# VectorE in written order during the preparation of a hybrid layer, with the steps of three triangular inversions dealt out anew

## The chip, the cores and the metric

One Trainium2 chip, one core. The metric is the device time of one execution in microseconds (us); lower is better. Engines are named as in the profile: PE is TensorE, DVE VectorE, ACT ScalarE, POOL GpSimd, SP SyncE (here only an issuer of DMAs).

## What is computed

One layer of a diffusion backbone on 512 latent and 256 context tokens, width 1024, float32: a normed and modulated input is projected and split into 8 heads of 2-D neighbourhood attention and 8 heads of a bidirectional RWKV-7 scan; both are joined, projected and added to the input; then comes a mixture of 32 experts, two per token. The reference has the scan as a recurrence over tokens, for both directions:

```python
def step(S, inp):
    r_t, w_t, kk_t, akk_t, k_t, v_t = inp
    S = (S * w_t[:, :, None, :]
         - jnp.einsum('bhvk,bhk->bhv', S, kk_t)[..., None] * akk_t[:, :, None, :]
         + v_t[..., None] * k_t[:, :, None, :])
    return S, jnp.einsum('bhvk,bhk->bhv', S, r_t)
...
yx = jnp.concatenate([na_x, rw_x], axis=-1) @ w_out
x = x + mod_x[2] * yx
hx2 = modulate(rmsnorm(x, norm2_g[l]), mod_x[3], mod_x[4])
x = x + mod_x[5] * hier_moe(hx2, ...)
```

## The kernel before

The scan is done in chunks of 64 tokens. Within a chunk the tokens are coupled through a 64x64 triangular matrix, which has to be inverted: its two 32x32 diagonal blocks by forward substitution on DVE, the block between them by two products on PE. There are 4 head pairs x 2 directions x 12 chunks = 96 such matrices, and they go in three batches of 32.

The program has stages: the norm (to about 50 us of the span), the preparation `rwkv_prep` (to about 425 us), the scan with the attention worked in between its steps, the output projection, and the experts (from about 716 us to the end), which stream their weights from memory.

`rwkv_prep` (line 580) loops over the head pairs p = 0 to 3 with `rw_pair` (line 655). A pair has four units U0 to U3 (direction and half of the tokens). For a unit, `decay` issues four matmuls (psg, paf), a tanh on ACT and a scan on DVE (sig); `decayed` multiplies on DVE (the tiles b, AR, BK, af) and POOL; `coupling` has 48 matmuls (pmg), whose results DVE and ACT copy to ND and NO. Ahead of the units stand two chains of small DVE operations for the norms of keys (sn, 12 of them) and of attention heads (nst, 15), and the tile kk. The stages n = 2 to 6 of a pair run the units staggered: at stage n, `coupling` of U(n-3), `decayed` of U(n-2), `decay` of U(n-1).

Between these, PE gets filler: the rest of the input projection (`other_prep`, line 560), as groups of matmuls ip and ipn. A tile's results are evacuated by ACT and by DVE (ks, rs, vs, rot), and its weights are split into two halves by ACT (whi) and POOL (wlo). `fill(us)` deals out matmuls of so many nominal us, from `FILLS[p][i]` at the places of pair p; what is left over runs at the start of the scan. The matmuls for the modulation vectors (pm, which wait for the weights wm) are dealt out among the filler; what is left of them comes before the third inversion, `s.all(s.mods)`.

An inversion is a generator, `solve_a` (line 793): transpose of ND to Mc, a copy Tc on ACT, 30 steps of two DVE operations each (tmp, then Tc += tmp, each on what the one before wrote, 30 to 240 columns), and two transposes Ta and Tn. While a filler is dealt out, `solve_on` (line 261) advances it by one step for every RATE[p] nominal us. The first batch is complete in pair 1 (stage 4), the second in pair 2 (stage 5), the third in pair 3 (stage 6). `solve_b` (line 822) runs what steps are left and issues the first product (pp<-Tn,NO); `solve_c` (line 839) issues the second, whose result TT goes to memory for the scan. `SOLVE_B` says at which pair and stage that happens for the first two batches.

Order: PE's matmuls of the preparation keep the order in which the code is written. For the other engines a scheduler chooses the order, unless the engine's name is in `s.ordered` (class `Ordered`, line 203), which pins each of its instructions to the written order. In the preparation `s.ordered = E1_ORD`, an empty tuple.

Of the kernel before, what the change touches and what calls it, by code (L numbers as in the profile page):

```python
# [8 lines left out]
F32 = mybir.dt.float32  # L9
# [64 lines left out]
def by_row(t):  # L74

    v = t[:, 0:512].rearrange("p (r c) -> p r c", c=64)
    return v[:, 0:4], v[:, 4:8][:, ::-1]


def by_tile(t):  # L80

    v = t.rearrange("p (k h c) -> p h k c", h=2, c=64)
    return v[:, 0], v[:, 1]
# [88 lines left out]

FILL = (2.2, 2.2, 2.66)
PRE = 8  
E1_ORD = ()
SCAN_ORD = ('vector',)
ORD_TO = 1
KP_AT = 2
END_ORD = ()
HT_DVE = (4, 6, 7)  # L180
START_FILL = (0, 12)
FILLS = ((17.23, 9.32, 4.14, 4.14, 4.14, 4.14, 6.22), (14.0, 9.0, 4.1, 4.7, 4.0, 4.0, 6.0), (14.0, 9.0, 4.1, 4.7, 4.0, 4.0, 6.0), (4, 3.13, 3, 2.72, 3.13, 3, 0.0))  
END_FILL = (4, 2)  
RATE = {1: 1.5, 2: 0.8}
SOLVE_B = {(2, 3): (0, 0), (2, 4): (0, 1), (3, 3): (1, 0), (3, 4): (1, 1)}
FIRST = ('k0', 'r0', 'v0')
ITEMS = (('k1', 'r1', 'v1', 'nk0'), ('k2', 'r2', 'v2', 'nq0'), ('k3', 'r3', 'v3', 'nv0'), ('nk1', 'gd', 'nq1', 'nv1'))  
MODGAP = 3.43  
H1 = (3, 2, 0)
UPE = lambda nc: nc.vector  # L190
LAST = 16  
OUT_ORD = ('scalar',)
MOE_ORD = ('vector',)
LAST_PARTS = (256, 256, 256, 256)
# [33 lines left out]
class K:  # L228
# [22 lines left out]
    def fill(s, us):  # L251

        while us > 0 and s.filler is not None:
            c = next(s.filler, None)
            if c is None:
                s.filler = None
                return
            us -= c
            s.solve_on(c)
# [320 lines left out]
    def rwkv_prep(s):  # L580
        tc, nc, L, PA = s.tc, s.nc, s.L, s.PA
        with tc.tile_pool(name="pb", bufs=1, side="right", reuse_waits="tile") as PB:
            s.PB = PB
            s.strict = True
            s.ordered = E1_ORD
            s.kt, s.rt, s.pend = {}, {}, None
# [21 lines left out]
            s.last = s.filler  # L608
            s.fill(LAST)
            s.solve_b()  # L610
# [44 lines left out]
    def rw_pair(s, p):  # L655

        nc, PB, prm = s.nc, s.PB, s.prm
        k, r = s.kt[p], s.rt[p]
        fill = lambda i: s.fill(FILLS[p][i])

        kkc = prm[:, P_KK + p:P_KK + p + 1]
        sq = PB.tile([128, TOK], F32, name="sq", bufs=2)
        s.act(sq, k, AF.Square, scale=kkc)

        rk = PB.tile([128, TOK], F32, name="sq", bufs=2)[:, 0:512]
        for o, a, b in zip(by_tile(rk), by_row(r), by_row(k)):
            nc.gpsimd.tensor_tensor(o, a, b, ALU.mult)
        U = [(d, hf) for d in range(2) for hf in range(2)]
        st = [s.decay(p, d, hf) for d, hf in U[:1]]
        pn = s.ps((128, 12), tag='pr', name="pnk")  # L670
        for i in range(6):
            s.mm(pn[:, 2 * i:2 * i + 2], sq[:, 128 * i:128 * i + 128], s.ctb[:, B_HONE:B_HONE + 2])
        sn = PB.tile([128, 36], F32, name="sn")
        nc.vector.tensor_scalar(sn[:, 12:24], pn, 1e-24, None, op0=ALU.max)
        s.rsqrt(sn[:, 0:12], sn[:, 12:24], sn[:, 24:36])
        rex = PB.tile([128, 6, 128], F32, name="sq", bufs=2)
        s.act(rex.rearrange("p i (h f) -> p (i h) f", f=64), sn[:, 0:12, None].to_broadcast([128, 12, 64]))
        fill(0)
        pb = s.ps((128, 8), tag='pr', name="pbo")
        for i in range(4):  # L680
            s.mm(pb[:, 2 * i:2 * i + 2], rk[:, 128 * i:128 * i + 128], prm[:, P_RK + 2 * p:P_RK + 2 * p + 2])
        nc.vector.tensor_copy(s.bonus[:, :, 2 * p:2 * p + 2], pb.rearrange("p (a b) -> p a b", b=2))
        p0, p1 = s.transposed(rex.rearrange("p a b -> p (a b)"), 'pr', "pr")
        kk = PB.tile([128, TOK], F32, name="kk")
        nc.vector.scalar_tensor_tensor(kk[:, 0:512], k[:, 0:512], kkc, p0, op0=ALU.mult, op1=ALU.mult)
        nc.vector.scalar_tensor_tensor(kk[:, 512:768], k[:, 512:768], kkc, p1, op0=ALU.mult, op1=ALU.mult)
        fill(1)

        ab = []
        for n in range(2, 7):  # L690
            i = n - 2
            if 1 <= i:
                s.coupling(p, *U[i - 1], *ab[i - 1])
            if i < 4:
                ab.append(s.decayed(p, *U[i], st[i], k, r, kk))
            if i < 3:
                st.append(s.decay(p, *U[i + 1]))
            if n == 6 and p == 3:
                s.all(s.mods)
                s.all(s.solve_a(p, s.NO))  # L700
                s.fill(sum(END_FILL))
            if (p, n) in SOLVE_B:
                b, half = SOLVE_B[p, n]
                if half == 0:
                    s.solve_b()
                s.solve_c(b, half)
            if n == 6 and p < 3:
                s.up_load(p + 1)
            fill(n)
        if p < 3:  # L710
            s.fill(1e9)
# [54 lines left out]
    def coupling(s, p, d, hf, AR, BK):  # L766
# [13 lines left out]
        while c < 6:  # L780
# [7 lines left out]
            if u0 + n == 32 and p < 3:  # L788
                s.solving, s.due, s.rate = s.solve_a(p, s.NO), 0.0, RATE[p]
                next(s.solving)  # L790
# [31 lines left out]
    def solve_b(s):  # L822

        PB = s.PB
        s.all(s.solving or ())
        s.solving = False
        NO, Ta, Tn = s.inverse
        lo, hi = s.LO, s.HI
        s.P1 = PB.tile([128, 32, 32], F32, name="P1", tag="Tc")
        for z in range(2):  # L830
            pq = s.ps(tag='pr', name="pp1")
            for k in range(16):
                u = 16 * z + k
                for h in range(2):
                    s.mm(pq[hi[h], 32 * k:32 * k + 32], NO[lo[h], u], Tn[lo[h], u])
            for h in range(2):
                s.act(s.P1[hi[h], 16 * z:16 * z + 16].rearrange("p u c -> p (u c)"), pq[hi[h], :])

    def solve_c(s, b, z):

        nc, PB = s.nc, s.PB
        NO, Ta, Tn = s.inverse
        P1, lo, hi = s.P1, s.LO, s.HI
        TT = PB.tile([128, 16, 64], F32, name="TT", tag="Mc" if b == 2 and z else "TT")

        g0, parts = 32 * b + 16 * z, []
        g = g0
        while g < g0 + 16:
            n = min(12 - g % 12, g0 + 16 - g)
            parts.append((g // 24, g // 12 % 2, g % 12, g - g0, n))  # L850
            g += n
        pq = s.ps(tag='pr', name="pp2")
        for p, d, a, k0, n in parts:
            src = Tn if d else Ta
            ro = hi if d else lo
            for k in range(k0, k0 + n):
                u = 16 * z + k
                for h in range(2):
                    l, r = (Ta, P1) if d else (P1, Ta)
                    s.mm(pq[ro[h], 32 * k:32 * k + 32], l[hi[h], u], r[hi[h], u])  # L860
            us, ks = slice(16 * z + k0, 16 * z + k0 + n), slice(k0, k0 + n)
            for q in range(4):
                rr, o = slice(32 * q, 32 * q + 32), 32 * (q % 2)
                s.act(TT[rr, ks, o:o + 32], src[rr, us])
                if q % 2 != d:
                    nc.gpsimd.memset(TT[rr, ks, 32 - o:64 - o], 0.0)
        for p, d, a, k0, n in parts:
            ro, ks = hi if d else lo, slice(k0, k0 + n)
            for h in range(2):
                s.act(TT[ro[h], ks, (0 if d else 32):(32 if d else 64)],  # L870
                      pq[ro[h], 32 * k0:32 * k0 + 32 * n].rearrange("p (u c) -> p u c", c=32))
        for p, d, a, k0, n in parts:
            for x, y in s.runs(d, a, a + n, d):
                (s.nc.scalar if b == 2 else s.nc.sync).dma_start(s.at(s.TT, d, x, y)[:, :, d, p].rearrange("c p f -> p c f"),
                                                                 TT[:, k0 + x - a:k0 + y - a])
# [1153 lines left out]
```

## Time and profile before

| what | value |
|---|---|
| median of 3 runs | 1200.48 us (1197.87, 1200.48, 1200.89) |
| profiled execution, its own time | 1198.07 us |
| its span (the time axis of the trace) | 1196.3 us |
| mean granted clock of PE, 1.0 is full | 0.951 |
| busy share of the span: PE, DVE, ACT, POOL | 91%, 53%, 34%, 21% |
| memory read | 283.22 MB |

The busy share is a mean over stages with different limits. In this program it says little on the preparation, where PE, DVE and POOL hand work to each other, so the profile is read by stretches of time and by what each engine waited for.

### The profile page before, as it was taken

How to read it: one execution, taken by the hardware profiler on the slowest of the kernel's cores; microseconds unless marked ns; L12 is line 12 of the kernel's file. 1: busy time of each engine (PE TensorE's matmuls, PEld its weight loads, DVE VectorE, ACT ScalarE, POOL GpSimd, SP SyncE). 2: the span in 40 equal slices, each digit the busy share in tenths (PEclk: the TensorE clock that was granted, in tenths of full speed). 3: DMA queues.
4: the chain of work that ended last, by engine and by line, in shares of the span. 5: the costliest groups of instructions: out<-in, count | busy, mean ns of one | idle time of the engine just before them, and what ended most of it. 6: DMA issues, size and time to landing. Idle time of an engine off the chain costs nothing.

```text
span 1196.3 us, 23890 instructions
## 1 busy us (share of the span) xinstructions
PE 1091.7 (91%) x9673; PEld 762.6 (64%) x9674; DVE 633.8 (53%) x1384; ACT 403.2 (34%) x780; POOL 247.0 (21%) x283
## 2 busy tenths in 40 slices
PE   3899999969587689999998979999999999999996
PEld 1677777748466678888776754646464646464644
DVE  5745567986938523554578782333333333333335
ACT  3543546347373534555322251111111111120200
POOL 0664465524334100020253030000000000000000
PEclk9999999979878787999999989999999999999998
DMA  9544655446434278764353939999999999999995
GB/s 370 174 132 142 192 188 178 144 129 186 136 87 166 68 213 225 220 179 107 103 144 119 364 123 365 409 409 409 408 409 409 408 409 408 409 409 409 407 409 188
DMA packets 148797, 310.00 MB, mean 259 GB/s; under 512 B 32323, under 2 KB 71107, under 8 KB 148684
## 3 DMA queue, kind: packets, MB, share of 16 engines
q1 hardware_dynamic: 142860, 305.82, 71.4%
q10 hardware_dynamic: 5792, 2.62, 0.8%
q8 instruction: 77, 1.26, 0.4%
q14 instruction: 36, 0.29, 0.1%
q0 software_dynamic: 32, 0.00, 0.0%
HBM read 283.22 MB, written 25.17 MB: 258 GB/s over the span
## 4 chain that ended last, share of the span: by engine, by line
PE 65%; DVE 19%; DMA 7%; ACT 4%; issue 2%; POOL 2%; SPq 0%; ACTq 0%; DVEq 0%; POOLq 0%
PE ph L244 16%; PE py L244 8%; PE psc L244 7%; PE ip L244 7%; PE pga L244 4%; DMA wt<-in_w_dram 4%; PE ipn L244 4%; DVE Tc L213 4%; DVE tmp L213 3%; PE pgr L244 3%; PE pr L244 2%; PE pm L244 1%; PE ppt L248 1%; PE pon L244 1%; ACT TT L213 1%
## 5 line engine op out<-in xcount | busy, mean ns | idle before, releaser
L244 PE MATMUL ph<-wt,HS 128*64 128x512 f32 x1024 | 224.6, 593 | 0.4 <-DMA wt<-in_w_dram 0.2
L244 PEld LDWEIGHTS ph<-wt,HS 128*64 128x64 f32 x1024 | 73.5, 137 | 140.7 <-issue 126.4
L213 DVE TENSOR_TENSOR hid<-hid,ph 128x512 f32<-128x512 f32 x16 | 11.0, 688 | 249.6 <-PE ph L244 249.6
L244 PE MATMUL py<-wt,hid 128*64 128x256 f32 x1024 | 114.5, 381 | 0.0
L244 PEld LDWEIGHTS py<-wt,hid 128*64 128x64 f32 x1024 | 71.9, 137 | 40.3 <-issue 3.9
L213 POOL CAST two<-sel 128x128 fp32r<-128x128 f32 x32 | 8.6, 296 | 425.4 <-PE pbc L244 425.4
L213 POOL TENSOR_TENSOR wlo<-wraw,whi 128x512 fp32r<-128x512 f32 x54 | 72.4, 1343 | 111.4 <-ACT whi L213 107.7
L244 PE MATMUL ipn<-whi,hth 128*128 128x256 f32 x256 | 82.2, 321 | 13.6 <-DVE vs L213 9.9
L213 DVE TENSOR_TENSOR x<-psc,x 128x512 f32<-128x512 f32 (+1 forms) x136 | 78.6, 650 | 0.0
L244 PE MATMUL ipn<-wlo,hth 128*128 128x256 f32 x256 | 77.4, 302 | 0.0
L244 PE MATMUL ipn<-whi,htl 128*128 128x256 f32 x256 | 76.8, 300 | 0.0
L244 PE MATMUL ip<-hth,whi 128*128 128x512 f32 (+1 forms) x200 | 74.7, 374 | 1.4 <-ACT nr L213 1.3
L244 PE MATMUL ip<-htl,whi 128*128 128x512 f32 (+1 forms) x200 | 71.3, 357 | 0.7 <-DVE htl L213 0.7
L244 PE MATMUL ip<-hth,wlo 128*128 128x512 f32 (+1 forms) x200 | 71.3, 356 | 0.0
L244 PEld LDWEIGHTS ipn<-whi,hth 128*128 128x128 f32 x256 | 54.1, 211 | 22.2 <-issue 19.4
L244 PE MATMUL pga<-OH,xh 128*128 128x256 f32 x240 | 60.1, 291 | 0.9 <-DVE OH L213 0.9
L244 PE MATMUL pga<-OH,xl 128*128 128x256 f32 x240 | 59.2, 287 | 0.0
L244 PE MATMUL psc<-yh,oht 128*128 128x512 f32 (+1 forms) x136 | 54.5, 405 | 1.2 <-DVE x L213 0.8
L213 ACT ACTIVATE hid<-pth 128x512 f32<-128x512 f32 x16 | 9.6, 599 | 133.3 <-PE pth L248 133.3
L244 PEld LDWEIGHTS ipn<-wlo,hth 128*128 128x128 f32 x256 | 54.2, 212 | 0.0
L244 PEld LDWEIGHTS ipn<-whi,htl 128*128 128x128 f32 x256 | 54.2, 212 | 0.0
L244 PE MATMUL psc<-yl,oht 128*128 128x512 f32 (+1 forms) x136 | 51.4, 381 | 0.1
(351 smaller groups left out, 2235.9 us busy)
## 6 DMA issues: line engine op xcount, KB each, us to landing
wt<-in_w_dram SPq DMA_DIRECT2D x384, 512.0 KB
wm<-in_wmod_dram SPq DMA_DIRECT2D x48, 512.0 KB
wraw<-in_w_in_dram SPq DMA_DIRECT2D x30, 256.0 KB
wraw<-in_w_na_dram SPq DMA_DIRECT2D x24, 256.0 KB
BKj<-BKd SPq DMA_DIRECT2D x12, 512.0 KB
BKd<-BK SPq DMA_DIRECT2D x12, 384.0 KB
ARz<-ARd SPq DMA_DIRECT2D x16, 256.0 KB
wo<-in_w_out_dram SPq DMA_DIRECT2D x16, 256.0 KB
```

The source lines that it names most:

```text
L213: i = f(*a, **k)
L244: i = s.nc.tensor.matmul(out, l, r, start=start, stop=stop)
L248: i = s.nc.tensor.transpose(out, x, s.ident if ident is None else ident)
```

## The change

Five edits, none of which adds or takes away a computation:

- `E1_ORD` becomes `('vector',)`: DVE keeps the written order through the whole preparation.
- `RATE` becomes 1.2 for the first inversion (it was 1.5), stays 0.8 for the second, and gets an entry 0.7 for the third. The third inversion was issued as a whole at stage 6 of pair 3; now its steps are dealt out between fillers as those of the other two.
- `SOLVE_B`: the products of the second inversion move from stages 3 and 4 of pair 3 to stages 5 and 6.
- `FILLS[3]`: the first two fillers of pair 3 grow from 4 and 3.13 to 8 and 4 nominal us; `LAST`, the filler before the last product, shrinks from 16 to 12.
- `solve_b` keeps Ta, Tn and its product in `s.halved`, where `solve_c` reads them, since the third inversion may now start before the second's last product is made.

```diff
-E1_ORD = ()
+E1_ORD = ('vector',)
...
-FILLS = (..., (4, 3.13, 3, 2.72, 3.13, 3, 0.0))
+FILLS = (..., (8, 4, 3, 2.72, 3.13, 3, 0.0))
 END_FILL = (4, 2)
-RATE = {1: 1.5, 2: 0.8}
-SOLVE_B = {(2, 3): (0, 0), (2, 4): (0, 1), (3, 3): (1, 0), (3, 4): (1, 1)}
+RATE = {1: 1.2, 2: 0.8, 3: 0.7}
+SOLVE_B = {(2, 3): (0, 0), (2, 4): (0, 1), (3, 5): (1, 0), (3, 6): (1, 1)}
...
-LAST = 16
+LAST = 12
...
             if n == 6 and p == 3:
                 s.all(s.mods)
-                s.all(s.solve_a(p, s.NO))
+                s.all(s.solving or ())
+                s.solving, s.due, s.rate = s.solve_a(p, s.NO), 0.0, RATE[p]
+                next(s.solving)
                 s.fill(sum(END_FILL))
...
     def solve_b(s):
...
-        s.P1 = PB.tile([128, 32, 32], F32, name="P1", tag="Tc")
+        P1 = PB.tile([128, 32, 32], F32, name="P1", tag="Tc")
+        s.halved = Ta, Tn, P1
...
     def solve_c(s, b, z):
...
-        NO, Ta, Tn = s.inverse
-        P1, lo, hi = s.P1, s.LO, s.HI
+        Ta, Tn, P1 = s.halved
+        lo, hi = s.LO, s.HI
```

What this moves is seen in the order of instructions on the engines. First DVE in pair 2, where the results of the projection tile v (vs) are taken out of PE's accumulators while the first inversion runs (the last number of a row is the shape; a step's size tells which of the 30 it is). Before:

```order
L213 TENSOR_TENSOR tmp<-Mc,Tc 128x108
L213 SCALAR_TENSOR_TENSOR vs<-ip,prm,vs 128x511
L213 TENSOR_TENSOR Tc<-Tc,tmp 128x4x27
L213 SCALAR_TENSOR_TENSOR vs<-ip,prm,vs 128x511
L213 SCALAR_TENSOR_TENSOR b_2810<-af,kk 128x384
L213 SCALAR_TENSOR_TENSOR sig<-cut,sig 128x390
L213 SCALAR_TENSOR_TENSOR vs<-ip,prm,vs 128x255
L213 TENSOR_TENSOR tmp<-Mc,Tc 128x84
L213 SCALAR_TENSOR_TENSOR vs<-ip,prm,vs 128x255
```

With the change:

```order
L213 TENSOR_TENSOR Tc<-Tc,tmp 128x7x24
L213 SCALAR_TENSOR_TENSOR b_2707<-af,kk 128x384
L213 SCALAR_TENSOR_TENSOR AR<-kk,Ep 128x6x64
L213 SCALAR_TENSOR_TENSOR BK<-b_2707,Em 128x6x64
L213 TENSOR_TENSOR af<-af,ks 128x384
L213 SCALAR_TENSOR_TENSOR sig<-cut,sig 128x390
L213 SCALAR_TENSOR_TENSOR vs<-ip,prm,vs 128x511 x2
L213 SCALAR_TENSOR_TENSOR vs<-ip,prm,vs 128x255 x2
L213 TENSOR_TENSOR tmp<-Mc,Tc 128x150
```

The four vs operations stood after the first operation of the step with 108 columns (the 27th); now they stand after the step with 168 columns (the 24th), but behind b, AR, BK, af of U0 and the scan sig of U1, and nothing stands between them.

Next DVE where the first inversion ends (Ta, Tn), at stage 3 of pair 2. Before:

```order
L213 TENSOR_TENSOR tmp<-Mc,Tc 128x30
L213 TENSOR_TENSOR Tc<-Tc,tmp 128x30
L213 STREAM_TRANSPOSE Ta<-Tc 128x32x32
L213 TENSOR_TENSOR ND<-pmg,ctb 128x192
L213 STREAM_TRANSPOSE Tn<-Tc 128x32x32
L213 SCALAR_TENSOR_TENSOR b_3072<-af,kk 128x384
L213 SCALAR_TENSOR_TENSOR sig<-cut,sig 128x390
```

With the change:

```order
L213 SCALAR_TENSOR_TENSOR AR<-kk,Ep 128x6x64
L213 SCALAR_TENSOR_TENSOR BK<-b_2825,Em 128x6x64
L213 TENSOR_TENSOR af<-af,ks 128x384
L213 SCALAR_TENSOR_TENSOR sig<-cut,sig 128x390
L213 TENSOR_TENSOR tmp<-Mc,Tc 128x84
L213 TENSOR_TENSOR Tc<-Tc,tmp 128x3x28
L213 TENSOR_TENSOR tmp<-Mc,Tc 128x58
L213 TENSOR_TENSOR Tc<-Tc,tmp 128x2x29
L213 TENSOR_TENSOR tmp<-Mc,Tc 128x30
L213 TENSOR_TENSOR Tc<-Tc,tmp 128x30
L213 STREAM_TRANSPOSE Ta<-Tc 128x32x32
L213 STREAM_TRANSPOSE Tn<-Tc 128x32x32
L213 TENSOR_TENSOR ND<-pmg,ctb 128x192
```

Before, the last steps and Ta stood ahead of ND of unit U0, and Tn right behind it. Now ND of U0 comes first, three steps and both transposes come last, and b, AR, BK, af of U1 and sig of U2 stand between.

Then PE in pair 3, at the first products of the second inversion (pp<-Tn,NO). Before:

```order
L244 MATMUL pmg<-AR,BK 32x64 x24
L244 MATMUL psg<-th_538,uph 128x384
L244 MATMUL psg<-th_538,upl 128x384
L244 MATMUL paf<-ad_613,uph 128x384
L244 MATMUL paf<-ad_613,upl 128x384
L244 MATMUL pp_3713<-Tn,NO 32x32 x32
L244 MATMUL pp_3748<-Tn,NO 32x32 x32
L244 MATMUL pp_3784<-Ta,P_3712 32x32 x8
L244 MATMUL pp_3784<-P_3712,Ta 32x32 x24
```

With the change:

```order
L244 MATMUL ip<-hth_111,wlo 128x512
L244 MATMUL pmg<-BK,AR 32x64 x24
L244 MATMUL pp_3961<-Tn,NO 32x32 x32
L244 MATMUL pp_3996<-Tn,NO 32x32 x32
L244 MATMUL pp_4032<-Ta,P_3960 32x32 x8
L244 MATMUL pp_4032<-P_3960,Ta 32x32 x24
L244 MATMUL ip<-hth_112,whi 128x512
```

The products stood behind pmg of unit U0 and the matmuls of `decay` for U2; now they stand behind pmg of U2, two stages later. Of the pm matmuls that were left over before the third inversion, a quarter has moved up among the fillers.

## Rows read from the trace of the kernel before

**Rows 1.** The page: the chain that ended last, share of the span by engine.

```profile
PE 65%; DVE 19%; DMA 7%; ACT 4%; issue 2%; POOL 2%; SPq 0%; ACTq 0%; DVEq 0%; POOLq 0%
```

**Rows 2.** Windows: stretch, its length, busy of PE, PEld, DVE, ACT, POOL; PEclk, DMA share, GB/s.

```profile
198.70:252.90 54.20, 44.91 (x361) 35.43 (x360) 52.97 (x110) 24.63 (x52) 28.25 (x27) 0.91 0.55 169
252.90:264.50 11.60, 8.34 (x81) 6.04 (x81) 11.43 (x21) 3.70 (x8) 1.65 (x3) 0.66 0.37 106
284.40:332.40 48.00, 31.09 (x297) 26.60 (x295) 46.26 (x102) 20.49 (x43) 17.12 (x25) 0.82 0.50 152
332.40:366.40 34.00, 27.30 (x514) 20.26 (x514) 11.65 (x25) 21.28 (x45) 12.29 (x22) 0.80 0.39 114
366.40:403.50 37.10, 28.75 (x191) 26.14 (x189) 35.49 (x80) 12.83 (x23) 13.38 (x11) 0.87 0.29 100
448.10:462.10 14.00, 14.00 (x138) 12.54 (x140) 3.38 (x10) 5.01 (x10) 0.00 (x0) 0.50 0.96 240
720.00:960.00 240.00, 239.25 (x1472) 132.09 (x1470) 84.14 (x137) 37.20 (x66) 4.28 (x16) 1.00 1.02 407
```

**Rows 3.** Waits of PE, whole span: us in total, times, longest.

```profile
PE pp L244 <- DVE Tn L213: 14.8, 2, 13.9
PE ipn L244 <- DVE vs L213: 9.9, 2, 9.7
PE pp L244 <- DVE nst L213: 5.7, 1, 5.7
PE pm L244 <- DMA wm<-in_wmod_dram: 4.2, 2, 3.5
PE pon L244 <- DMA V<-NVd: 3.9, 3, 1.8
...
PE pr L248 <- ACT sq L213: 3.1, 1, 3.1
```

**Rows 4.** Timeline of PE: start, duration, instruction, in brackets the wait before it.

```profile
254.66 0.55 PE L244 MATMUL ipn<-whi,hth 128*128 128x256 f32 x1 [9.75 <-DVE vs L213]
...
264.55 1.64 PE L244 MATMUL pp<-Tn,NO 32*32 32x32 f32 x92 [0.89 <-DVE Tn L213]
...
283.04 0.87 PE L244 MATMUL pmg<-BK,AR 64*32 64x64 f32 x48
...
332.54 1.67 PE L244 MATMUL pp<-Tn,NO 32*32 32x32 f32 x55 [13.95 <-DVE Tn L213]
```

**Rows 5.** Timeline of DVE at the first inversion's end.

```profile
254.89 0.97 DVE L213 TENSOR_TENSOR_SCAN sig<-cut,sig 128x390 f32<-128x390 bf16 x1
...
260.26 2.00 DVE L213 STREAM_TRANSPOSE Ta<-Tc 128x1024 f32<-128x1024 f32 x1
...
262.51 1.98 DVE L213 STREAM_TRANSPOSE Tn<-Tc 128x1024 f32<-128x1024 f32 x1
264.37 0.56 DVE L213 SCALAR_TENSOR_TENSOR b<-af,kk 128x384 f32<-128x384 f32 x1
```

**Rows 6.** Timeline of DVE, 216 to 305 us: start, duration, instruction; two mixed, two dependent.

```profile
217.47 0.37 DVE L213 TENSOR_TENSOR tmp<-Mc,Tc 128x210 f32<-128x210 f32 x1
217.76 0.17 DVE L213 TENSOR_TENSOR nst<-nst 128x16 f32<-128x16 f32 x1
...
304.62 0.41 DVE L213 TENSOR_TENSOR Tc<-Tc,tmp 128x240 f32<-128x240 f32 x1
305.06 0.41 DVE L213 TENSOR_TENSOR tmp<-Mc,Tc 128x240 f32<-128x240 f32 x1
```

**Rows 7.** Timelines of DVE and POOL, 244 to 251 us: start, duration, instruction.

```profile
247.59 1.31 DVE L213 TENSOR_TENSOR Tc<-Tc,tmp 128x198 f32<-128x198 f32 x1
...
250.26 0.35 DVE L213 TENSOR_TENSOR Tc<-Tc,tmp 128x184 f32<-128x184 f32 x1
...
247.30 2.72 POOL L213 TENSOR_TENSOR wlo<-wraw,whi 128x512 fp32r<-128x512 f32 x2
```

**Rows 8.** Groups of DVE, 366 to 403 us: instruction, count, busy us, mean ns, idle before.

```profile
L213 DVE SCALAR_TENSOR_TENSOR rot<-ip,prm,rot 128x511 f32<-128x511 f32 x2 | 1.5, 740 | 0.0
```

More of the change, by code (lines that the diff above doesn't have):

```diff
@@ L181 @@
 START_FILL = (0, 12)
-FILLS = ((17.23, 9.32, 4.14, 4.14, 4.14, 4.14, 6.22), (14.0, 9.0, 4.1, 4.7, 4.0, 4.0, 6.0), (14.0, 9.0, 4.1, 4.7, 4.0, 4.0, 6.0), (4, 3.13, 3, 2.72, 3.13, 3, 0.0))
+FILLS = ((17.23, 9.32, 4.14, 4.14, 4.14, 4.14, 6.22), (14.0, 9.0, 4.1, 4.7, 4.0, 4.0, 6.0), (14.0, 9.0, 4.1, 4.7, 4.0, 4.0, 6.0), (8, 4, 3, 2.72, 3.13, 3, 0.0))
 END_FILL = (4, 2)
-RATE = {1: 1.5, 2: 0.8}
-SOLVE_B = {(2, 3): (0, 0), (2, 4): (0, 1), (3, 3): (1, 0), (3, 4): (1, 1)}
+RATE = {1: 1.2, 2: 0.8, 3: 0.7}
+SOLVE_B = {(2, 3): (0, 0), (2, 4): (0, 1), (3, 5): (1, 0), (3, 6): (1, 1)}
 FIRST = ('k0', 'r0', 'v0')
@@ L836, in solve_b @@
             for h in range(2):
-                s.act(s.P1[hi[h], 16 * z:16 * z + 16].rearrange("p u c -> p (u c)"), pq[hi[h], :])
+                s.act(P1[hi[h], 16 * z:16 * z + 16].rearrange("p u c -> p (u c)"), pq[hi[h], :])
     def solve_c(s, b, z):
         nc, PB = s.nc, s.PB
-        NO, Ta, Tn = s.inverse
-        P1, lo, hi = s.P1, s.LO, s.HI
+        Ta, Tn, P1 = s.halved
+        lo, hi = s.LO, s.HI
         TT = PB.tile([128, 16, 64], F32, name="TT", tag="Mc" if b == 2 and z else "TT")
```

## The prediction

> **What bounds the kernel.** I read the page first: the chain that ended last runs over PE for 65% of it, DVE for 19% and DMA for 7% [rows 1]. A share says nothing on where, so the table of windows comes next. In the experts' stage DMA is occupied throughout at 407 GB/s (share 1.02) [rows 2]: its length is given by the bytes, nothing there can absorb or repay a delay, and what the preparation gains or loses arrives at the end. In the preparation the table of waits shows what PE lacked. The largest have DVE at their end: 14.8 us for Tn, 9.9 us for vs, 5.7 us for what the profile calls nst (Tn of the third inversion ends beside it) [rows 3]. The reader is to see in the windows that DVE is full just there: 52.97 of 54.2 us in the stretch that holds the first inversion, 46.26 of 48.0 in the second, 35.49 of 37.1 in the third [rows 2]. So the change is priced at the places where PE waits for DVE: what stands ahead of the awaited instruction in DVE's stream before, and what with the change. Durations are those of the profiled execution, 1198.07 us.
>
> **Evacuation of vs, pair 2.** PE waits 9.75 us, until 254.66 [rows 4]. DVE never rests, so the wait moves by the work put ahead of vs. The scheduler had run ahead to the 27th step by then; in written order DVE does the 24 that the fillers have dealt out. Two whole steps less are four operations near 0.4 us, -1.6. The written order puts b, AR, BK, af of one more unit behind Mc, where the scheduler had them before it: four operations, b lasting 0.56 us [rows 5], starts some 0.5 apart, +2.1; the scan of U1 (0.97) stands ahead now, +1.0. The third part is lost mixing. A step's operations depend on each other: tmp of 305.06 starts 0.03 us after Tc ended at 305.03. Independent ones overlap: nst of 217.76 starts 0.08 us before tmp ends [rows 6]. Before, 27 small operations (sn, nst) stood between steps and cost little more than the overlap left open; in written order they are a chain of their own, at 0.17 us each and the gap about 0.2 us, 5.4 in all. About half of that was paid before: +2.5. The first result is +4.0. DVE is also held up by POOL here (a step's operation takes 1.31 us while wlo is made on POOL and 0.35 when it is over [rows 7]), and which steps meet it will change; six such collisions, about 1 us each, either way give -2 to +10.
>
> The Trainium skill (VectorE: DVE Perf Modes, section "The DRAIN you can't avoid") says that the pipeline empties behind each DVE operation before the next one starts, and that chaining without waits does not avoid it. By that mixing never saved anything, and the term of 2.5 (and its like below) would be zero. The trace does not agree in full: the mixed operations do overlap by 0.08 us [rows 6].
>
> **First inversion's end, stage 3 of pair 2.** Before, PE's first product waited only 0.89 us [rows 4], since the scheduler put Tn (262.51) right behind ND and left sig of U2 to follow. With the written order ND of U0 comes, which needs pmg, then b, AR, BK, af of U1 (2.1), sig of U2 (1.0, after its tanh), the last three steps (six operations of 30 to 84 columns, where one of 210 takes 0.37 [rows 6]: some 0.25 each with the gaps, 1.5), Ta 2.00 and Tn 1.98 [rows 5], all in front of PE's product, which itself stands ahead of all later PE work. Sum from 262.6: 8.5 us, Tn ends at about 271, the product starts at about 271 where it was 264.55: +6.4. If sig runs while b to af do not hold it up and mixing costs nothing, +4; with POOL in the way, +8.
>
> **From pair 2's third unit to the third inversion.** This stretch runs from pmg at 283.04 [rows 4] to the first step at 366.4: the windows of 48.0 and 34.0 us. PE is busy 31.09 + 27.30 = 58.4, DVE 46.26 + 11.65 = 57.9 of these 82 us [rows 2]; neither fills it, the hand-offs do. Before, PE stood 13.95 us ahead of the second product [rows 4] and 3.1 ahead of pr (for sq and the sn chain behind it) [rows 3]. The product now stands behind pmg of U2, and the larger fillers stand where PE had run dry, so these 17.05 go. New waits come: pmg of U0 needs AR and BK, which now stand behind the steps dealt out before them (3.2 in my walk of both streams), pmg of U2 the same (3.5), and Tn stands behind the nst chain, two units' groups and a scan (2.4): 9.1. Mixing lost between steps and small operations is another 3. -17.05 + 9.1 + 3 = -5.0. The ends: if PE gets no new wait, what is gained is 17.05 less the added filler, 4.87 nominal us, -12; if every wait returns in another place, +2. The DMA waits of pm, 4.2 [rows 3], stay, since the rest of pm still stands behind the last unit.
>
> **Third inversion.** It was issued as a whole, but its fillers ran beside it, and DVE was full for 35.49 of 37.1 us [rows 2]; dealing its steps out cannot shorten it. The evacuations rot and gs of tile gd move ahead (rot 1.5 us for its two operations [rows 8], gs, half as wide, some 0.6: -2.1); the nst chain of tile nq1 now stands in the middle of the steps and waits for PE and ACT there (+2). Net 0, with ends -2 and +3. PE has 4 nominal us less to do meanwhile, so its wait for the last Tn grows from 5.7 to 10 or more; that lies beside DVE's work, which sets the end.
>
> **The scan's start.** The left-over filler stands before the first scan products, no longer partly behind; nothing is saved in work, but V, for which PE waited 3.9 us [rows 3], is asked for later relative to its store. Behind those waits PE ran at a granted clock of 0.50, the 1.2 GHz level, for 14.0 us [rows 2]; at 2.4 GHz this would be at most 7.0 shorter. So the relief lies between 0 and 3.9 + 7.0, some -10; I take -4: most of the waits, little of the clock.
>
> **The clock elsewhere.** Around the wait for vs the granted clock was 0.66 [rows 2]. Longer idle stretches before the first product cost a little more of this: +1 (0 to +3). Pairs 0 and 1 have no PE wait of note: 0. The `s.halved` edit issues nothing.
>
> **Sum.** 4.0 + 6.4 - 5.0 + 0 - 4.0 + 1.0 = +2.4, hence 1198.07 + 2.4 = 1200.5. The profiled execution lies 2.4 us under the median of the three runs, 1200.48, and near their lowest, so the forecast is no difference that can be measured: 0.3%, 3.6 us, is about what a measurement of this kernel tells from no change (1196.9 to 1204.1).
>
> **Rivals.** First, faster: *V and the clock.* If V arrives in time the scan's start goes at full clock (-10 instead of -4), and if pair 3's new waits stay small (-9 instead of -5), the sum is -7.6: 1190.5. For it: two of the largest waits end in one place, pair 3, and PE's product is moved away from there. Against: what PE no longer waits for there it waits for elsewhere, since DVE's work is the same. Chance 0.23.
>
> Second, faster: *unmixing is free.* Then 2.5 and 3 fall out: 1198.07 - 3.1 = 1195.0. For it: the scheduler's order was no optimum, it ran steps ahead of vs. Against: the 0.08 us overlaps. The rule of the Trainium skill quoted above (VectorE: DVE Perf Modes) would give this time. Chance 0.12.
>
> Third, slower: *head of line in pair 2.* In written order one instruction that waits for PE or ACT stops DVE, which in turn is what PE waits for; each such stop in the two stages around the first inversion's end costs both. It decides if ND or sig blocks before the steps are done: vs +9, first product +8, pair 3 at -5, the scan at -4, clock +2: +10, 1208. Against: rate 1.2 leaves only three steps there. Chance 0.22.
>
> Fourth, *no effect*: the order pinned is what ran already; excluded in pair 2 by the order shown, but the gains and losses may cancel to within a microsecond, 1200. Chance 0.05.
>
> **How the numbers follow.** The forecast has 0.38: 0.27 in the band, 0.06 faster, 0.05 slower. The two fast rivals add 0.23 and 0.12, of the latter 0.02 in the band; the slow one 0.22; no effect 0.05 in the band. Faster 0.39, same 0.34, slower 0.27. The terms' half-widths (6, 2, 7, 2.5, 5, 1.5) taken as independent give 11; so 1188 to 1211, which holds the fast rivals and the slow one.
>
> **What would show it.** Right: PE's wait for vs in pair 2 near 14 us; a wait of 6 to 8 us ahead of pp<-Tn in pair 2; no wait near 14 in pair 3, but two or three of 2 to 4; the third inversion still near 37 us with DVE full; a wait of PE of 10 or more at its end; waits for V under 3.9. Wrong, if vs is taken out earlier than before, if the first product finds Tn ready, or if the third inversion's steps start later than they did.

## The result, and the profile after

The changed kernel takes 1231.05 us (median of 4 runs, 1229.2 to 1237.2), the kernel before 1200.68 (median of 4 runs beside them). The ratio is 1.026, with a 95% interval of 1.022 to 1.031: slower by 2.6%, some 31 us. The forecast was no difference, 1200.5, in a range to 1211.

The page's row on busy time:

```profile
PE 1090.1 (89%) x9673; PEld 761.2 (62%) x9674; DVE 634.5 (52%) x1384; ACT 402.2 (33%) x780; POOL 247.1 (20%) x283
```

PE's busy time is what it was (1090.1 us; 1091.7 before); its share fell because the span grew to 1227.4. So no work was added; what came on top is waits. The table of what PE waited for (us in total, times, longest):

```profile
PE pp L244 <- DVE Tn L213: 23.0, 3, 12.7
PE psg L244 <- DVE upl L213: 15.9, 3, 6.6
...
PE ipn L244 <- DVE vs L213: 11.6, 3, 10.1
PE pmg L244 <- DVE BK L213: 11.4, 2, 9.2
PE pm L244 <- DMA wm<-in_wmod_dram: 8.3, 1, 8.3
PE pnt L248 <- ACT nx L213: 6.3, 1, 6.3
```

Against [rows 3]: Tn costs 23.0 us where it was 14.8, and in three places. The wait for vs is nearly the same. Two entries are new, 15.9 us for upl and 11.4 for BK; the wait for wm (4.2 before) and that for nx ahead of the scan (pnt, 3.2 before) have doubled. Where the lag comes about is seen when the same instruction is looked up in both timelines:

| instruction | before | after | lag |
|---|---|---|---|
| PE: pnk of pair 1 | 151.39 | 159.79 | 8.4 |
| PE: pnk of pair 2 | 210.41 | 229.02 | 18.6 |
| PE: first ipn behind vs, pair 2 | 254.66 | 275.22 | 20.6 |
| PE: first product of the first inversion | 264.55 | 292.34 | 27.8 |
| PE: pmg of U2, pair 2 | 283.04 | 312.77 | 29.7 |
| PE: pnk of pair 3 | 293.55 | 326.91 | 33.4 |
| DVE: first step of the third inversion | 366.36 | 401.23 | 34.9 |
| PE: first product of the third inversion | 403.53 | 437.99 | 34.5 |
| PE: first matmul of the experts (ph) | 716.34 | 747.16 | 30.8 |

18.6 of the 31 us are there at pnk of pair 2, before the first place that the prediction priced. The places in PE's timeline (start, duration, instruction, in brackets the wait before it):

```profile
150.99 0.44 PE L244 MATMUL psg<-th,uph 128*128 128x384 f32 x1
...
157.94 0.69 PE L244 MATMUL psg<-th,upl 64*128 64x384 f32 x1 [6.50 <-DVE upl L213]
...
159.79 2.72 PE L244 MATMUL pnk<-ctb,sq 128*128 128x2 f32 x12
...
227.17 0.69 PE L244 MATMUL psg<-th,upl 64*128 64x384 f32 x1 [6.57 <-DVE upl L213]
...
275.22 0.55 PE L244 MATMUL ipn<-whi,hth 128*128 128x256 f32 x1 [10.11 <-DVE vs L213]
...
292.34 3.46 PE L244 MATMUL pp<-Tn,NO 32*32 32x32 f32 x122 [8.71 <-DVE Tn L213]
...
373.94 1.51 PE L244 MATMUL pmg<-BK,AR 64*32 64x64 f32 x48 [9.22 <-DVE BK L213]
...
398.38 1.08 PE L244 MATMUL pm<-wm,scc 128*32 128x256 f32 x8 [8.35 <-DMA wm<-in_wmod_dram]
...
437.99 3.46 PE L244 MATMUL pp<-Tn,NO 32*32 32x32 f32 x122 [12.71 <-DVE Tn L213]
```

The two matmuls of `psg` stand one behind the other, and the second, whose weights are upl, waits 6.5 us at the boundary from pair 0 to 1 and 6.57 at the next. Behind these waits PE runs slower: `pnk`, 12 small matmuls, takes 2.72 us, where it took 1.50 at both places before; the granted clock from 157.94 to 165.00 us is 0.50, the 1.2 GHz level, and was 1.00 from 140.0 to 150.5.

Why upl is late is seen on DVE, at the boundary from pair 0 to pair 1:

```profile
150.73 0.69 DVE L213 TENSOR_REDUCE nst<-nx 128x8 f32<-128x512 f32 x1 [0.88 <-ACT nx L213]
151.73 1.28 DVE L213 TENSOR_REDUCE nst<-nx 128x8 f32<-128x512 f32 x2 [0.32 <-ACT nx L213]
153.05 1.49 DVE L213 TENSOR_SCALAR nst<-nst 128x24 f32<-128x24 f32 x3
...
156.41 0.35 DVE L213 TENSOR_TENSOR ND<-pmg,ctb 128x192 f32<-128x192 f32 x1
156.67 2.40 DVE L213 TENSOR_TENSOR upl<-row,uph 64x256 fp32r<-64x256 f32 x2
```

nst, the chain of a norm of the attention heads, started once ACT had its input (nx), and its first operations are to be seen here. Behind it come ND of U3 (156.41) and upl (156.67). In the code the filler whose last tile needs that norm stands at stage 5 and `up_load` at stage 6, and the order of DVE is now the code's. In the kernel before, the scheduler had made upl 7 us ahead of PE's use of it at 150.28:

```profile
142.34 0.86 DVE L213 TENSOR_TENSOR upl<-row,uph 64x256 fp32r<-64x256 f32 x2
```

At the next boundary it had made it just in time: the two operations of upl, one for each direction, ran from 207.62 to 209.43 us, and PE's first matmul with upl started at 209.30 without a wait.

The windows of the stretches of [rows 2], here from 208.5 to 437.95 (columns as there):

```profile
208.50:273.50 65.00, 47.84 (x361) 37.77 (x360) 55.50 (x110) 26.11 (x53) 26.82 (x26) 0.82 0.41 132
273.50:292.30 18.80, 8.41 (x81) 6.28 (x81) 13.57 (x25) 5.83 (x13) 5.11 (x7) 0.59 0.37 109
312.70:401.20 88.50, 65.46 (x832) 52.27 (x830) 66.49 (x132) 46.96 (x95) 34.68 (x43) 0.80 0.49 147
401.20:437.95 36.75, 23.84 (x233) 22.32 (x232) 32.87 (x76) 8.40 (x17) 11.25 (x16) 0.83 0.20 58
```

The stretch that holds the first inversion's steps up to vs, 54.2 us before, takes 65.0, and DVE is busy for 55.50 of it, where it was for 52.97: it is not full any more, it waits. (This stretch contains the boundary to pair 2.) The granted clock is 0.82 there (0.91 before) and 0.59 from vs to the first product. The third inversion takes 36.75 us as against 37.1, with DVE at 32.87.

### The profile page after: what moved, and what is told of

Same layout as the page of the kernel before. It is cut to its first block, busy times and chain, and to the rows that moved or that the text cites. A ratio compares the mean times of both kernels' runs of the same rounds, so it can differ in the third digit from the quotient of the medians.

```text
span 1227.4 us, 23886 instructions
## 1 busy us (share of the span) xinstructions
PE 1090.1 (89%) x9673; PEld 761.2 (62%) x9674; DVE 634.5 (52%) x1384; ACT 402.2 (33%) x780; POOL 247.1 (20%) x283
## 4 chain that ended last, share of the span: by engine, by line
PE 44%; DMA 10%; DVE 5%; ACT 2%; SPq 1%; POOL 1%; issue 1%; ACTq 0%; DVEq 0%; POOLq 0%
PE ph L244 15%; PE py L244 7%; DMA wt<-in_w_dram 7%; PE psc L244 5%; PE pga L244 4%; PE pgr L244 2%; PE acc L244 2%; PE pr L244 1%; PE ppt L248 1%; PE pon L244 1%; PE po L244 1%; DMA V<-NVd 1%; DVE x L213 1%; SPq L213 1%; DVE fst L213 1%
## 5 line engine op out<-in xcount | busy, mean ns | idle before, releaser
L244 PE MATMUL ipn<-whi,hth 128*128 128x256 f32 x256 | 80.1, 313 | 12.1 <-DVE vs L213 11.6
L213 ACT ACTIVATE S<-S,m 128x512 f32<-128x512 f32 x64 | 45.3, 717 | 26.7 <-DVE m L213 26.6
```

The lines of the kernel that those rows point to most:

```text
L213: i = f(*a, **k)
L244: i = s.nc.tensor.matmul(out, l, r, start=start, stop=stop)
```

## The experiments

A ratio is the kernel's time over that of the kernel before on the same chip, with its 95% interval. Theory A says that the written order makes the loss, theory B that the redistribution of steps, products and fillers does. An inversion has a first and a second product; where an expectation writes "the second product", with its wait of 14 us, the first product of the second inversion is meant (13.95 us before, [rows 4]).

**The order alone.** The kernel before, and in it only

```diff
-E1_ORD = ()
+E1_ORD = ('vector',)
```

> Kernel before with one edit: DVE in written order. Theory A (the written order itself makes the loss: small chains nst stand ahead of upl at the pair boundaries, b to sig ahead of Tn at the first inversion's end): slower by 22 to 40 us, 1223 to 1241, with waits of PE for upl near 15 us in all and a wait near 8 us at the first product; as the second product stays at its old place, its wait stays over 10 us. Theory B (the redistribution of steps, products and fillers makes the loss, the order little): within 5 us of before, no waits for upl.

Measured: 1250.24 us, ratio 1.039 (1.034 to 1.044). Slower still than the change, beyond theory A's range. Its waits of PE:

```profile
PE pp L244 <- DVE Tn L213: 29.4, 2, 17.3
PE ipn L244 <- DVE rot L213: 25.7, 1, 25.7
PE psg L244 <- DVE upl L213: 16.2, 3, 6.9
```

The waits for upl are there (16.2 us). The largest single one, 25.7 us for rot, was 2.5 before: rot is the evacuation of tile gd, in written order behind all steps of the third inversion, which this kernel issues as a whole. In the changed kernel rot is done at 385.95, ahead of the third inversion's transpose at 391.73, and PE does not wait for it. So by the traces the dealing out of the third inversion repairs there what the order would break; a run with the order and the dealing out alone was not made.

**All but the order.** The changed kernel with `E1_ORD = ()`.

> The change with the order of DVE left to the scheduler again, all else as changed. Theory A: 1193 to 1204, no waits of PE for upl, the first product waits under 2 us, and the wait of 14 us at the second product is mostly gone. Theory B: 1222 to 1231.

Measured: 1191.89 us, ratio 0.9925 (0.9896 to 0.9954). Faster than before, and 1 us under theory A's range. Theory A holds: against the change, the order costs 1231 - 1192 = 39 us, the rest of the change gains 9 without the order and 1250 - 1231 = 19 with it. Waits:

```profile
PE ipn L244 <- DVE vs L213: 10.5, 2, 10.3
PE pm L244 <- DMA wm<-in_wmod_dram: 9.3, 1, 9.3
PE pp L244 <- DVE Tn L213: 8.6, 1, 8.6
```

No wait for upl. The 8.6 us for Tn are not at the second inversion but at the third; the timeline shows the first products of both:

```profile
338.39 2.21 PE L244 MATMUL pp<-Tn,NO 32*32 32x32 f32 x128
...
398.17 3.46 PE L244 MATMUL pp<-Tn,NO 32*32 32x32 f32 x122 [8.56 <-DVE Tn L213]
```

So the wait of 14 us is gone, as expected, and PE does not wait at the first inversion's product either.

**upl a stage earlier**, in the changed kernel:

```diff
-            if n == 6 and p < 3:
+            if n == 5 and p < 3:
                 s.up_load(p + 1)
```

> The changed kernel with the low-rank weights of the next pair (uph, upl) prepared one stage earlier, at stage 5, so that upl stands ahead of the nst chain in DVE's written order. Theory A: the three waits of PE for upl, 15.9 us in all, go, and the idle clock behind them, so 1211 to 1217 (gain 14 to 20). Theory B, or a chain that holds PE anyway (sn and sig stand behind the same nst): the wait returns at pnk's users or at the next tile, 1226 to 1232.

Measured: 1220.02 us, ratio 1.0146 (1.0105 to 1.0187): 11 us gained by the medians and 14 by the ratios, at or below the low end of what was expected. The lag at pnk of pair 2 fell from 18.6 to 5.5 us (and pnk of pair 0 already lay 2.7 late in this execution), so the boundaries are repaired for the most part, but a little was given back behind them: the waits for vs and BK are 12.8 and 12.1 us, where they were 11.6 and 11.4.

```profile
PE ipn L244 <- DVE vs L213: 12.8, 3, 11.3
PE pmg L244 <- DVE BK L213: 12.1, 3, 9.2
```

**First products a stage later**, in the changed kernel:

```diff
-SOLVE_B = {(2, 3): (0, 0), (2, 4): (0, 1), (3, 5): (1, 0), (3, 6): (1, 1)}
+SOLVE_B = {(2, 4): (0, 0), (2, 5): (0, 1), (3, 5): (1, 0), (3, 6): (1, 1)}
```

> The changed kernel with both products of the first inversion one stage later (stages 4 and 5 of pair 2). Theory A: the 8.7 us wait ahead of the first product shrinks to under 2, 1222 to 1226. Rival: DVE was late for what stands behind as well, the wait returns at pmg of U1 or at the second inversion, 1229 to 1234.

Measured: 1228.03 us, ratio 1.0225 (1.0185 to 1.0265), between the two expectations: some 3 us, with an interval that overlaps that of the change. The first product still waits 7.14 us for Tn at its new place. At pmg of U1 the lag was 13.0 instead of 29.7 us (the products no longer stand ahead of it), at pmg of U2 25.5, at the experts' first matmul 28.2. The move passes the wait on.

**The inversion's end ahead of stage 3**, in the changed kernel, which keeps the products in their place:

```diff
             i = n - 2
+            if p == 2 and n == 3:
+                s.all(s.solving or ())
+                s.solving = False
             if 1 <= i:
```

What stands ahead of Tn on DVE in the changed kernel:

```profile
277.62 0.27 DVE L213 TENSOR_TENSOR Tc<-Tc,tmp 128x108 f32<-128x108 f32 x1
282.22 0.36 DVE L213 TENSOR_TENSOR ND<-pmg,ctb 128x192 f32<-128x192 f32 x1 [4.33 <-PE pmg L244]
...
284.89 0.96 DVE L213 TENSOR_TENSOR_SCAN sig<-cut,sig 128x390 f32<-128x390 bf16 x1
...
288.67 1.90 DVE L213 STREAM_TRANSPOSE Ta<-Tc 128x1024 f32<-128x1024 f32 x1
290.44 1.84 DVE L213 STREAM_TRANSPOSE Tn<-Tc 128x1024 f32<-128x1024 f32 x1
```

DVE had done the step with 108 columns at 277.9 and stood 4.33 us idle for ND, whose pmg was not there; sig, the last steps and both transposes could only follow.

> The changed kernel with the last three steps of the first inversion, Ta and Tn written ahead of stage 3's coupling in pair 2, so that they stand ahead of ND, b to af and sig on DVE. In the changed kernel's trace DVE stands 4.3 us idle ahead of that ND, for pmg, and then has 9.5 us of work before Tn ends. Theory (head of line): Tn ends some 1 to 2 us behind pmg, the wait of 8.7 us at the first product goes to under 1, 1221 to 1224. Rival: AR and BK of U1 and sig of U2 come late instead and PE waits for those: 1228 to 1233.

Measured: 1223.32 us, ratio 1.020 (1.017 to 1.022), some 8 us gained, as expected. PE:

```profile
279.02 0.55 PE L244 MATMUL ipn<-whi,hth 128*128 128x256 f32 x1 [10.14 <-DVE vs L213]
...
287.05 2.44 PE L244 MATMUL pp<-Tn,NO 32*32 32x32 f32 x128 [0.93 <-DVE Tn L213]
```

The product waits 0.93 us instead of 8.71, and the wait for vs ahead of it is still 10.14.

**Both repairs**, upl and the inversion's end.

> The changed kernel with both repairs: uph and upl a stage earlier, and the first inversion's end ahead of stage 3. If the two losses are separate: gains add, 11 + 8, 1210 to 1214. If the earlier lateness of one hides in the other's wait: 1215 to 1220.

Measured: 1210.31 us, ratio 1.009 (1.006 to 1.012). The gains add: 21 us by the medians and 20 by the ratios, where the two alone gave 11 + 8 and 14 + 8. What is left against the run without the order is 18 to 20 us; some 8 of it is the order from pair 3 on (below), the rest was not tried apart.

**The order by place.** In the changed kernel the order of DVE is kept for pairs 0 and 1 only, for pair 2 only, or from pair 3 on (`s.ordered` is set at the head of the loop over pairs).

> The change with DVE in written order in pairs 0 and 1 only. Theory A: the two boundaries with their waits for upl cost 18 us (trace: pnk of pair 2 comes 18.6 us late), nothing is repaid: 1191.9 + 18 = 1208 to 1213. Rival: lateness at a boundary is absorbed later by DVE's waits in pair 2 (vs, first product): 1195 to 1203.

> The change with DVE in written order in pair 2 only. The order costs 39 us in all (change against all but the order), 14.4 in pairs 0 and 1 and 8.2 from pair 3 on. If costs by place add up: 16.6 in pair 2, 1208 to 1211. If a late pair 2 is partly made good in pair 3 when that is free: 1197 to 1205. Trace: a wait near 8 us at the first product and, at the boundary to pair 3, a wait for upl.

> The change with DVE in written order from pair 3 on. By the traces of the change and of the run without the order, the lag grows by 7 us from pair 3's pnk to the end: 1196 to 1202. Rival: the lag in pair 3 is inherited from pair 2 and order in pair 3 is free or helps: 1188 to 1194.

Measured: 1206.3 us, ratio 1.004 (1.001 to 1.006), for pairs 0 and 1; 1202.19, ratio 1.002 (1.000 to 1.004), for pair 2; 1200.07, ratio 0.999 (0.996 to 1.001), from pair 3 on. Less the 0.9925 of the run without any order these are 0.011, 0.009 and 0.006, or 14, 11 and 8 us, together 32 of the 39 to 40. In pairs 0 and 1:

```profile
PE psg L244 <- DVE upl L213: 15.6, 2, 9.1
```

and from pair 3 on:

```profile
PE pp L244 <- DVE Tn L213: 14.3, 2, 12.7
...
PE pmg L244 <- DVE BK L213: 9.8, 2, 9.2
```

For pairs 0 and 1 the result lies a little under what the lag at pnk promised (18 us): there the lag is 22.0 us at pnk of pair 2 and 17.3 at the first ipn behind vs. While PE waited for upl, the scheduler's order let DVE get ahead with the steps (Tn of the first inversion ends only 3.8 us later than before), so that the wait for vs, near 10 us in most of the other kernels, shrank to 3.7. For pair 2 the second expectation came true, for pair 3 the first.

**The products of the second inversion alone**, in the kernel before, all else as there:

```diff
-SOLVE_B = {(2, 3): (0, 0), (2, 4): (0, 1), (3, 3): (1, 0), (3, 4): (1, 1)}
+SOLVE_B = {(2, 3): (0, 0), (2, 4): (0, 1), (3, 5): (1, 0), (3, 6): (1, 1)}
```

> Kernel before with the second inversion's products two stages later alone (old rates, fillers and LAST, third inversion in one go, DVE left to the scheduler). If the moved products make the gain of the redistribution: 1190 to 1195. If the dealt-out third inversion or the larger fillers make it: 1197 to 1203.

Measured: 1187.39 us, ratio 0.987 (0.984 to 0.990), the lowest of all, beyond the expected gain. Its profiled execution was the slowest of its six, 1192.13 us; PE's waits there:

```profile
PE pp L244 <- DVE Tn L213: 8.5, 2, 7.8
...
PE pm L244 <- DMA wm<-in_wmod_dram: 3.8, 2, 3.1
```

Where the second inversion's first product waited 13.9 us it now waits 7.8, the wait for wm stays near 4 (3.8, it was 4.2), and the third inversion's first product comes 5.6 us earlier than before (397.96).

**With the third inversion dealt out as well** (rate 0.7, fillers and LAST as before):

> The kernel with only the moved products (1187.4) plus the third inversion dealt out among its fillers at rate 0.7, DVE left to the scheduler. If dealing out is nothing where DVE sets the end: 1185 to 1190. If it is what separates 1187.4 from all but the order (1191.9): 1190 to 1194.

Measured: 1189.57 us, ratio 0.992 (0.990 to 0.994). The interval touches that of the products alone, 0.984 to 0.990, so it is not settled whether dealing out costs 2 to 6 us without the order, or nothing; no gain is seen. The lower rate of the first inversion and the larger fillers were not tried alone.

**No pm left before the third inversion.** With all of the change but the order, `MODGAP` goes from 3.43 to 3.15. In the changed kernel the last load of wm stood on SP's queue behind six stores of KTd, which took 7.59 us to issue, and the third inversion's steps waited for Tc, which in the code takes a buffer of wm and so has to wait for the pm that reads it:

```profile
386.80 7.59 SPq L213 DMA_DIRECT2D KTd<-nx  x6
394.49 0.41 SPq L213 DMA_DIRECT2D wm<-in_wmod_dram  x1
```

```profile
391.73 1.93 DVE L213 STREAM_TRANSPOSE Mc<-ND 128x1024 f32<-128x1024 f32 x1
401.23 0.20 DVE L213 TENSOR_TENSOR tmp<-Mc,Tc 128x30 f32<-128x30 f32 x1 [7.57 <-ACT Tc L213]
```

> All of the change but the order of DVE, and the modulation matmuls pm dealt out every 3.15 instead of 3.43 nominal us, so that none is left before the third inversion. Theory: in the run without the order PE waits 9.3 us there for the last wm load, which stands on SP behind six KTd stores, and the third inversion's first step waits 7.9 us with it; without that the third inversion starts 6 to 9 us earlier: 1182 to 1187. Rival: the third inversion is held by something else (rot and gs, ND), or earlier pm wait for their weights elsewhere: 1189 to 1194.

Measured: 1191.44 us, ratio 0.992 (0.989 to 0.995): no gain. The wait for wm is gone, but PE waits for ARz (1.0 us in the run without the order) and uph instead; the one for Tn was there already:

```profile
PE pgr L244 <- DMA ARz<-ARd: 9.6, 2, 8.5
PE pp L244 <- DVE Tn L213: 7.9, 1, 7.9
...
PE psg L244 <- ACT uph L213: 3.3, 1, 3.3
```

PE waits for uph at the boundary to pair 3 and for ARz at the scan's start. The third inversion did not start earlier: its transpose Mc starts at 364.91 us and its first step at 368.15, where they were at 355.11 and 364.91 in the run without the order. So the time lies in the rival's range and the load no longer holds the steps; what made Mc late was not traced.

## Why the prediction was wrong

- **Pairs 0 and 1: "no PE wait of note: 0".** This step failed. The prediction took from the waits of before that nothing is short there, and looked only at the instructions for which PE waited before. What had to be read is which instruction the scheduler had pulled ahead of others: upl lay 7 us ahead of its use at the first boundary and just ahead of it at the second, with the nst chain behind it. The written order puts nst first, and PE stands 6.5 us at each of the two, then runs at the lower clock. Cost: 18.6 us of lag by the trace; 14 us when made alone, 11 to 14 us gained when undone.
- **Evacuation of vs, +4.0.** The lag grew from 18.6 to 20.6 us: 2.0 in the trace, and the wait of PE is 10.1, not 14. This term was too large. It was sized by the sum of the work put ahead, on the ground that DVE is full, and DVE was no longer full; how much of each part reached PE was not tried apart. The wait itself hardly grew (9.75 to 10.11 us): from pnk of pair 2 to this place PE was busy for 36.09 us with the same matmuls, where it was 34.20 before; its granted clock there fell from 0.88 to 0.83.
- **First inversion's end, +6.4.** Right in mechanism and size: the wait is 8.71 us and the lag grew by 7.2; the run with the steps written ahead takes it away. From ND to the end of Tn DVE took 10.1 us, where 8.5 were priced. The 4.33 us of idle in front of ND, in which the last steps could have run, stood in the slow rival only.
- **From pair 2's third unit to the third inversion, -5.0.** Failed. The lag grew from 29.7 to 34.9, +5.2. Of the 17.05 us 15.4 went as said (13.95 became 1.62 at the second inversion's first product, and the 3.1 for sq are gone), and the moved products do gain (14 us alone), but new waits came: 9.22 us for BK at pmg of U2 (3.5 was priced), 8.3 for wm instead of a constant 4.2, and a third boundary, where the lag rose from 30.0 at pmg of U3 to 33.4 at pnk. The wait for wm was set to stay, without a look at SP's queue, where the load now came behind the stores. And a later start of the third inversion's steps was one of the prediction's own signs of being wrong.
- **Third inversion, 0.** Right: 36.75 us against 37.1, PE's wait at its end 12.7 us. DVE was less full than said, 32.87 us of it.
- **Scan's start, -4.0.** Right in sign and size: between the third inversion's first product and ph the lag fell by 3.6 us, and PE no longer waits for V (3.9 before); which part of it V makes and which the clock was not tried apart, so this step's mechanism is not shown.
- **The clock elsewhere, +1.0.** Behind the first product the lag grew by 1.9 us to pmg of U2: 1.3 us of it are the product's 122 matmuls, which took 3.46 us, where they took 2.12. That the pairs 0 and 1 would lose clock as well was missed with their waits.
- **The slow rival** was the one that came about: head of line, where one instruction that waits for another engine holds up all behind it on DVE. It had the mechanism but priced it at two stages of pair 2 only; the boundaries, of which there are three, were missing: so 10 us, and 1208, where 31 came.

The Trainium skill (VectorE: DVE Perf Modes, "The DRAIN you can't avoid") says that the next operation does not start until the pipeline is empty, but also that one that is not held starts earlier; the prediction took the first half alone. The overlap of 0.08 us in [rows 6] goes with the second half. The rival built on free unmixing had the kernel at 1195, and it came to 1231; what lost mixing costs by itself no run shows. The loss came from waits, not from the operations' length: DVE's busy time is 634.5 us as against 633.8.

## What to carry to other kernels

In written order an instruction whose input comes from elsewhere holds up all that stands behind it on its engine, wanted or not: here ND held the last steps for 4.33 us, and nst held upl. So, before pinning an order, list for each hand-off what the scheduler had pulled ahead, also where the profile of before shows no wait; the missing waits are its work. With the order pinned, a chain that waits for another engine's result (nst) is better written behind the short operations that others wait for; moving upl ahead of it gained 11 to 14 us here. And where a change has several parts, the sum hides them: here a part that gains 14 us alone (the moved products) came with one that costs 39 (the order).

## What was not expected of the hardware

The waits for upl were followed by matmuls at the lower of PE's two levels: psg of 384 columns takes 0.69 us behind the first of them and 0.44 before it, and the granted clock behind it is 0.50. So a wait cost more than its length. From pmg of U0 in pair 0, where the lag was 1.1 us, to pnk of pair 2 it grew by 17.5 us. The windows of this stretch, before and with the change (columns as in [rows 2]):

```profile
130.58:210.41 79.83, 77.45 (x847) 62.00 (x846) 51.47 (x101) 46.34 (x92) 46.38 (x49) 0.98 0.63 191
```

```profile
131.66:229.02 97.36, 80.47 (x846) 63.87 (x846) 58.66 (x116) 49.04 (x96) 48.91 (x51) 0.90 0.54 166
```

PE's idle time rose from 2.4 to 16.9 us (the two waits for upl and one of 2.19 for BK make 15.3 of it), and its busy time for the same matmuls from 77.45 to 80.47: 14.5 us of the lag are idle time, and 3.0 are matmuls at the lower clock.
